# Ten weight subtractions move to GpSimd and the softmax's division to ScalarE, in a two-layer diffusion trunk

## The chip, the cores and the metric

One core of a Trainium2 chip runs the whole program. The metric is the time of one execution in device microseconds; the kernel before takes 1686.2 us as the median of three runs (1684.12 to 1688.48). Engines are named as in the profile: PE is TensorE (PEld its weight loads), DVE is VectorE, ACT is ScalarE, POOL is GpSimd, SP is SyncE, which here issues the DMAs.

## What is computed

Two layers work on 256 latent and 256 context tokens of width 1024. Each layer is a half-step SwiGLU feed-forward, a token mixer, and another half-step feed-forward, each behind an RMSNorm that is modulated by a conditioning vector. The change lies in the mixer:

```python
ux = modulate(rms_norm(h, norm_g[l, 1]), mx[:, 3], mx[:, 4])     # latent; uc: the same for context
px = ux @ w_in[l]                                                # one projection for all head groups
...
mix_x = concatenate([
    multiscale_pool(px[..., :HYENA_OFF], ...),                   # 256 wide: pooling
    hyena_mixer(px[..., HYENA_OFF:Q_OFF], ...),                  # 256 wide: long convolution
    blocked_attention(qx, k_all, v_all),                         # 8 heads of 64, 2 key/value heads
]) @ w_out[l]
...
def attend(q, k, v):
    s = einsum('bqkgd,bskd->bkgqs', q, k) * ATTN_SCALE
    p = softmax(s, axis=-1)
    o = einsum('bkgqs,bskd->bqkgd', p, v)
```

Latent queries attend to latent and context keys (512), context queries to context keys alone (256). In the last layer the context's own mixer output is not needed, so that only its keys and values are made.

## The kernel before

Products are made exact to about fp32 from three faster ones (`mm3`, lines 58 to 65): each operand is held as a high part and a low part (operand minus high part), and PE runs high x high, high x low and low x high into one PSUM bank. For weights, `Stream` does this on the way (lines 95 to 132). SP loads a unit of 128x1024 into one of three `raw` tiles (wr, line 107), ACT copies it rounded into one of four `whi` tiles (wh, line 117), DVE subtracts into one of three `wlo` tiles (wl, line 122), and then the load four units further on is issued. `ahead` and `take` say how far this runs ahead of the matmuls. There are 310 such units; those of the input projection follow `JOBS[l]`: three Hyena blocks whose projection is the `head` (line 418), and behind them q, k and v blocks ("qkv", two units each), the remaining Hyena blocks and the two pooling blocks (`bulk`, line 935).

In the head, the matmuls over the modulated activations run first over the first stream of tokens and then over the second. Their high parts yhb are made on ACT (line 341) and their low parts ylb on DVE (line 348). Where a mixer begins, POOL writes the tables of the rotary positions, tab0 and tab1 (line 707), each in three sets of four operations.

Behind the head run the Hyena convolutions (to_time with its copies u and x on ACT, line 776; U, Y, Ye, yo, lines 785 to 839), the norms and rotations of q and k (hsqq, hqq, hrq, lines 873 to 895, on DVE), the pooling sums on POOL (lines 739 to 757) and attention (line 1006). One item of attention is one head and 128 queries: PE makes the scores S (line 966), DVE the negated row maximum (mx, line 973), ACT the exponential with the row sums (e and sm, line 976), DVE the reciprocal and the division in place (lines 980 and 981), PE four or two transposes (St, line 986), ACT one half of the copy out of PSUM and DVE the other (pT, lines 991 and 993), PE the products with v (po, line 999), and ACT and DVE split them into high and low. An item's exponential, the division of the item before it and the transposes of the item four earlier stand together in the code.

Inside the mixers a scheduler sets the order of the instructions on each engine from its own estimates; head and tails are ordered by hand. Each engine works through its own instructions strictly in that order. Layer 0 has 32 items (16 with 512 keys, 16 with 256), layer 1 has 16 with 512.

Of the kernel before, what the change touches and what calls it, by code (L numbers as in the profile page):

```python
# [11 lines left out]
F32 = mybir.dt.float32  # L12
F32R = mybir.dt.float32r
I32 = mybir.dt.int32
AF = mybir.ActivationFunctionType
ALU = mybir.AluOpType
# [3 lines left out]
P = 128  # L20
# [13 lines left out]
def hymba(ctx: ExitStack, tc: tile.TileContext, io: dict, out: bass.AP):  # L34
    nc = tc.nc
# [59 lines left out]
    class Stream:  # L95


        def __init__(self, units):
            self.units = units
            self.raw, self.hi, self.lo = [], [], []  # L100
            self.taken = 0

# [7 lines left out]
        def ahead(self, n, more=0):  # L110

            end = min(self.taken + n + more, len(self.units))
            for i in range(len(self.hi), end):
                self.load(i + 1)
                m = self.units[i].shape[-1]
                hi = wp.tile([P, 1024], F32R, tag="whi", name=f"wh{i}", bufs=4)
                nc.scalar.activation(hi[:, :m], self.raw[i][:, :m], AF.Copy)  # L117
                self.hi.append(hi)
            for i in range(len(self.lo), min(self.taken + n, len(self.units))):
                m = self.units[i].shape[-1]  # L120
                lo = wp.tile([P, 1024], F32R, tag="wlo", name=f"wl{i}", bufs=3)
                self.last = nc.vector.tensor_tensor(lo[:, :m], self.raw[i][:, :m], self.hi[i][:, :m].bitcast(F32), ALU.subtract)  # L122
                self.lo.append(lo)
                self.load(i + 4)

# [522 lines left out]
    def mixers(l, nrm, fill):  # L648
# [329 lines left out]

        def normalise(e, sm, nk):
            nc.vector.reciprocal(sm, sm)  # L980
            nc.vector.tensor_scalar(e[:, :nk * P], e[:, :nk * P], sm, None, ALU.mult)

        def transposed(e, pT, nm, qb, nk):
            ps = bank(f"St{nm}")
# [21 lines left out]
        def attention(heads):  # L1006
# [10 lines left out]
            for i in range(len(items) + depth + 1):  # L1017
                if i < len(items):
                    yield from need("k", f"q{items[i][0]}")
                    if i % 2 == 0:  # L1020
                        j, s, a, qb, keys = items[i]
                        pss = scores(j, s, qb, keys)
                    es[i] = softmax(pss[i % 2], *items[i])
                if 0 < i <= len(items):
                    normalise(*es[i - 1], len(items[i - 1][4]))
                for d in due:
                    values(*d)
                due = []
                if 0 <= i - depth < len(items):
                    j, s, a, qb, keys = items[i - depth]  # L1030
                    nk = len(keys)
                    if (j, s) not in pTs:
                        pTs[j, s] = [[big(f"pT{l}{j}{s}{b}{n}") for n in range(nk // 2)] for b in range(2)]
                    transposed(es.pop(i - depth)[0], pTs[j, s][a], f"{l}{j}{s}{a}{qb}", qb, nk)
                    if a == 1 and qb == 1:
                        due.append((j, s, keys, pTs[j, s]))
                yield
# [25 lines left out]
    def mix_out(l, mix, S, nxt, fill):  # L1063
# [17 lines left out]
    JOBS = (  # L1081
        [("hy", 2), ("hy", 3), ("hy", 4), ("hy", 5), ("qkv", 1), ("qkv", 0), ("qkv", 2), ("hy", 6), ("hy", 7), ("pool", 0), ("pool", 1)],
        [("hy", 2), ("hy", 3), ("hy", 4), ("qkv", 0), ("hy", 5), ("qkv", 1), ("qkv", 2), ("hy", 6), ("hy", 7), ("pool", 1), ("pool", 0)],
    )
    NB0 = 6
    units = []
    for l in range(DEPTH):
        for s in range(2):
            units += [io["w_gu"][l, s, f, a] for f in range(NF) for a in range(2)][0 if l or s else NB0:]
            units += [io["w_down"][l, s, m, :, a * P:b * P] for m in range(KB) for a, b in ((0, 8), (8, 15), (15, NF))]  # L1090
            if s == 0:
                for kind, b in JOBS[l]:
                    units += [io["w_qkv"][l, b, i] for i in range(2)] if kind == "qkv" else [io["w_feat"][l, b]]
                units += [io["w_out"][l, m] for m in range(KB)]
    weights = Stream(units)

    def start():

# [336 lines left out]
```

## Time and profile before

| | |
|---|---|
| runs, median (lowest, highest) | 1686.2 us (1684.12, 1688.48) |
| the profiled execution, its time and its span | 1689.82 us, 1688.0 us |
| PE, DVE, ACT, POOL busy | 1640.8, 1168.9, 873.1, 91.9 us |
| mean granted clock of PE | 0.989 |

The chain of work that ended last gives PE 86% and DVE 10% of the span. In a timeline a row is a run of instructions of one kind: when it starts, how long it lasts, and in brackets how long its engine stood idle before it and which instruction let it go. In a window row each engine has its busy time in that stretch and its number of instructions; PEclk is the granted clock, 1.00 being full speed. The mixers of layer 0 lie between about 430 and 580 us, those of layer 1 between about 1355 and 1463.

### The profile page before, as it was taken

How to read it: one execution, taken by the hardware profiler on the slowest of the kernel's cores; microseconds unless marked ns; L12 is line 12 of the kernel's file. 1: busy time of each engine (PE TensorE's matmuls, PEld its weight loads, DVE VectorE, ACT ScalarE, POOL GpSimd, SP SyncE). 2: the span in 40 equal slices, each digit the busy share in tenths (PEclk: the TensorE clock that was granted, in tenths of full speed). 3: DMA queues.
4: the chain of work that ended last, by engine and by line, in shares of the span. 5: the costliest groups of instructions: out<-in, count | busy, mean ns of one | idle time of the engine just before them, and what ended most of it. 6: DMA issues, size and time to landing. Idle time of an engine off the chain costs nothing.

```text
span 1688.0 us, 24751 instructions
## 1 busy us (share of the span) xinstructions
PE 1640.8 (97%) x9162; PEld 1398.6 (83%) x9162; DVE 1168.9 (69%) x2107; ACT 873.1 (52%) x1881; POOL 91.9 (5%) x120
## 2 busy tenths in 40 slices
PE   7999999999999999999999999999999995999999
PEld 5687788888897698888888898888888895789999
DVE  5688778666789767767633368777765698776653
ACT  3576567655424635656522236666655543454442
POOL 0222200000102100000000000000000012000000
PEclk9999999999999999999999999999999998999999
DMA  9455455555421024545433325555555452345564
GB/s 337 129 186 185 135 189 188 172 171 168 142 75 40 24 76 139 173 153 169 158 89 101 95 73 188 176 185 187 174 164 155 133 184 82 125 150 180 184 185 139
DMA packets 80121, 251.50 MB, mean 149 GB/s; under 512 B 8641, under 2 KB 14145, under 8 KB 80001
## 3 DMA queue, kind: packets, MB, share of 16 engines
q1 hardware_dynamic: 80000, 249.93, 45.9%
q8 instruction: 72, 1.18, 0.3%
q14 instruction: 49, 0.39, 0.1%
HBM read 246.75 MB, written 3.15 MB: 148 GB/s over the span
## 4 chain that ended last, share of the span: by engine, by line
PE 86%; DVE 10%; ACT 1%; issue 1%; DMA 1%; POOL 1%; SPq 0%; ACTq 0%; DVEq 0%; POOLq 0%
PE fp L63 15%; PE fp L64 15%; PE fp L65 15%; PE fd L63 7%; PE fd L65 7%; PE fd L64 7%; PE fp L429 2%; DVE wl L122 1%; PE po L999 1%; PE op L63 1%; PE op L64 1%; PE op L65 1%; PE St L986 1%; PE ip L429 1%; PE qp L862 1%
## 5 line engine op out<-in xcount | busy, mean ns | idle before, releaser
L117 ACT ACTIVATE wh<-wr 128x1024 fp32r<-128x1024 f32 (+1 forms) x310 | 320.6, 1036 | 483.3 <-PE fp L64 171.9
L122 DVE TENSOR_TENSOR wl<-wr,wh 128x1024 fp32r<-128x1024 f32 (+1 forms) x310 | 371.4, 1199 | 215.4 <-PE fd L65 92.8
L63 PE MATMUL fp<-yha,wh 128*128 128x512 f32 x632 | 251.0, 397 | 0.0
L65 PE MATMUL fp<-yha,wl 128*128 128x512 f32 x632 | 247.0, 391 | 0.0
L64 PE MATMUL fp<-yla,wh 128*128 128x512 f32 x632 | 247.0, 391 | 0.0
L63 PE MATMUL fd<-gh,wh 128*128 128x512 f32 (+1 forms) x616 | 223.3, 362 | 0.0
L64 PE MATMUL fd<-gl,wh 128*128 128x512 f32 (+1 forms) x616 | 223.3, 362 | 0.0
L65 PE MATMUL fd<-gh,wl 128*128 128x512 f32 (+1 forms) x616 | 223.3, 362 | 0.0
L63 PE MATMUL fp<-yhc,wh 128*128 128x512 f32 (+1 forms) x656 | 220.5, 336 | 0.0
L64 PE MATMUL fp<-ylc,wh 128*128 128x512 f32 (+1 forms) x656 | 220.4, 336 | 0.0
L65 PE MATMUL fp<-yhc,wl 128*128 128x512 f32 (+1 forms) x656 | 220.4, 336 | 0.0
L202 ACT ACTIVATE mt<-mt 128x512 f32<-128x512 f32 x240 | 149.9, 626 | 127.1 <-DVE mt L201 124.8
L201 DVE TENSOR_TENSOR mr<-mr,cb 128x512 f32<-128x512 f32 x240 | 159.7, 706 | 0.0
L201 DVE TENSOR_TENSOR mt<-mr,cb 128x512 f32<-128x512 f32 x240 | 159.6, 702 | 0.0
L202 ACT ACTIVATE mr<-mr 128x512 f32<-128x512 f32 x240 | 147.7, 617 | 5.3 <-DVE mr L201 5.0
L63 PEld LDWEIGHTS fp<-yha,wh 128*128 128x128 f32 x632 | 119.3, 189 | 30.2 <-issue 2.0
L64 PEld LDWEIGHTS fp<-yla,wh 128*128 128x128 f32 x632 | 119.3, 189 | 26.4 <-issue 1.9
L65 PEld LDWEIGHTS fp<-yha,wl 128*128 128x128 f32 x632 | 119.2, 189 | 25.1
L65 PEld LDWEIGHTS fp<-yhc,wl 128*128 128x128 f32 x656 | 124.5, 190 | 12.9
L64 PEld LDWEIGHTS fp<-ylc,wh 128*128 128x128 f32 x656 | 124.5, 190 | 12.7
L63 PEld LDWEIGHTS fp<-yhc,wh 128*128 128x128 f32 x656 | 124.5, 190 | 12.6
L65 PEld LDWEIGHTS fd<-gh,wl 128*128 128x128 f32 x616 | 116.3, 189 | 18.1
(521 smaller groups left out, 2640.1 us busy)
## 6 DMA issues: line engine op xcount, KB each, us to landing
wr<-in_w_gu SPq DMA_DIRECT2D x170, 512.0 KB, 3.5
mr<-in_w_modT SPq DMA_DIRECT2D x120, 512.0 KB, 3.5
wr<-in_w_down SPq DMA_DIRECT2D x64, 448.0 KB, 3.4
wr<-in_w_down SPq DMA_DIRECT2D x32, 512.0 KB, 3.6
m0w<-in_w_mod SPq DMA_DIRECT2D x32, 256.0 KB, 5.6
wr<-in_w_feat SPq DMA_DIRECT2D x16, 512.0 KB, 3.7
wr<-in_w_out SPq DMA_DIRECT2D x16, 512.0 KB, 3.4
wr<-in_w_qkv SPq DMA_DIRECT2D x12, 512.0 KB, 3.7
```

The source lines that it names most:

```text
L63: nc.tensor.matmul(ps, w[0], x[0], start=start, stop=False)
L64: nc.tensor.matmul(ps, w[0], x[1], start=False, stop=False)
L65: nc.tensor.matmul(ps, w[1], x[0], start=False, stop=stop)
L117: nc.scalar.activation(hi[:, :m], self.raw[i][:, :m], AF.Copy)
L122: self.last = nc.vector.tensor_tensor(lo[:, :m], self.raw[i][:, :m], self.hi[i][:, :m].bitcast(F32), ALU.subtract)
L201: nc.vector.tensor_tensor(ta, ra, cb[:, c, a * 512:(a + 1) * 512], ALU.mult)
L202: nc.scalar.activation(ta, ta, AF.Copy, accum_out=acc[:, k, c, a:a + 1])
L429: nc.tensor.matmul(pss[b][:, cols(s)], w[:, k * P:(k + 1) * P], y[k][p[1]][:, cols(s)], start=(p == HH and k == 0), stop=(b in last and k ...
L862: nc.tensor.matmul(o_, x[0][:, ct], w[1][:, cw], start=False, stop=(k == KB - 1))
L986: nc.tensor.transpose(ps[:, i * P:(i + 1) * P], e[:, i * P:(i + 1) * P], ident)
L999: nc.tensor.matmul(po[a * HD:(a + 1) * HD, :SEQ], att["v"][:, kb, a * HD:(a + 1) * HD], pT[a][n // 2][:, cols(n % 2)], start=(n == 0), sto ...
```

## The change

Two things. `Stream` gets a set `beside` of unit numbers whose low part is subtracted on POOL in place of DVE. The set holds every second unit of the input projection behind the head, five a layer: qkv 1a, qkv 0a, qkv 2a, hy 6 and pool 0 in layer 0, qkv 0b, qkv 1a, qkv 2a, hy 6 and pool 1 in layer 1. And the division of the softmax (48 items) becomes a copy on ACT whose scale is the reciprocal column; the reciprocal stays on DVE.

```diff
--- before.py
+++ after.py
@@ -95,8 +95,10 @@
     class Stream:
 
 
-        def __init__(self, units):
+
+        def __init__(self, units, beside):
             self.units = units
+            self.beside = beside
             self.raw, self.hi, self.lo = [], [], []
             self.taken = 0
 
@@ -119,7 +121,10 @@
             for i in range(len(self.lo), min(self.taken + n, len(self.units))):
                 m = self.units[i].shape[-1]
                 lo = wp.tile([P, 1024], F32R, tag="wlo", name=f"wl{i}", bufs=3)
-                self.last = nc.vector.tensor_tensor(lo[:, :m], self.raw[i][:, :m], self.hi[i][:, :m].bitcast(F32), ALU.subtract)
+                if i in self.beside:
+                    nc.gpsimd.tensor_tensor(lo[:, :m], self.raw[i][:, :m], self.hi[i][:, :m].bitcast(F32), ALU.subtract)
+                else:
+                    self.last = nc.vector.tensor_tensor(lo[:, :m], self.raw[i][:, :m], self.hi[i][:, :m].bitcast(F32), ALU.subtract)
                 self.lo.append(lo)
                 self.load(i + 4)
 
@@ -978,7 +983,7 @@
 
         def normalise(e, sm, nk):
             nc.vector.reciprocal(sm, sm)
-            nc.vector.tensor_scalar(e[:, :nk * P], e[:, :nk * P], sm, None, ALU.mult)
+            nc.scalar.activation(e[:, :nk * P], e[:, :nk * P], AF.Copy, scale=sm)
 
         def transposed(e, pT, nm, qb, nk):
             ps = bank(f"St{nm}")
@@ -1084,15 +1089,18 @@
     )
     NB0 = 6
     units = []
+    beside = set()
     for l in range(DEPTH):
         for s in range(2):
             units += [io["w_gu"][l, s, f, a] for f in range(NF) for a in range(2)][0 if l or s else NB0:]
             units += [io["w_down"][l, s, m, :, a * P:b * P] for m in range(KB) for a, b in ((0, 8), (8, 15), (15, NF))]
             if s == 0:
+                n0 = len(units) + 3
+                beside.update(range(n0 + 1, n0 + sum(2 if kind == "qkv" else 1 for kind, _ in JOBS[l][3:]), 2))
                 for kind, b in JOBS[l]:
                     units += [io["w_qkv"][l, b, i] for i in range(2)] if kind == "qkv" else [io["w_feat"][l, b]]
                 units += [io["w_out"][l, m] for m in range(KB)]
-    weights = Stream(units)
+    weights = Stream(units, beside)
 
     def start():
```

The scheduler then sets a new order. On POOL at the start of layer 0's mixers (gs0q and gs0k are factors of the rope tables, tab0... the tables, pu a pooling buffer, wl a low part), before:

```order
47 L701 TENSOR_SCALAR gs0q<-mc_2_3813 128x128
48 L701 TENSOR_SCALAR gs0k<-mc_2_3813 128x128
49 L707 TENSOR_TENSOR tab0qcos<-mc_1_3812,gs0q 128x2x64 x4
50 L707 TENSOR_TENSOR tab0qsin<-mc_1_3812,gs0q 128x2x64 x4
51 L707 TENSOR_TENSOR tab0k<-mc_1_3812,gs0k 128x2x64 x4
52 L739 MEMSET pu_00_4890 128x8
53 L740 MEMSET pu_00_4890 128x8
```

and now:

```order
47 L706 TENSOR_SCALAR gs0q<-mc_2_3813 128x128
48 L706 TENSOR_SCALAR gs0k<-mc_2_3813 128x128
49 L125 TENSOR_TENSOR wl_4046<-wr_3834,wh_4040 128x1024
50 L712 TENSOR_TENSOR tab0qcos<-mc_1_3812,gs0q 128x2x64 x4
51 L712 TENSOR_TENSOR tab0qsin<-mc_1_3812,gs0q 128x2x64 x4
52 L712 TENSOR_TENSOR tab0k<-mc_1_3812,gs0k 128x2x64 x4
53 L125 TENSOR_TENSOR wl_4158<-wr_4044,wh_4095 128x1024
54 L125 TENSOR_TENSOR wl_4353<-wr_4099,wh_4291 128x1024
55 L125 TENSOR_TENSOR wl_4510<-wr_4240,wh_4461 128x1024
56 L125 TENSOR_TENSOR wl_4700<-wr_4410,wh_4633 128x1024
57 L744 MEMSET pu_00_4890 128x8
58 L745 MEMSET pu_00_4890 128x8
```

The subtraction wl_4046 stands ahead of the rope tables, four more behind them; in layer 1 wl_12177 stands in the same way ahead of tab1 and the four others behind.

On ACT in layer 1, where the Hyena convolution's input goes to the time layout (u and x are copies of the transposed tt1u and tt1x, wh the high copies of weights), before:

```order
1039 L117 ACTIVATE wh_12545<-wr_12440 128x1024
1040 L873 ACTIVATE hsqq_12500<-qp_1_0_12448 128x512
1041 L117 ACTIVATE wh_12600<-wr_12446 128x1024
1042 L117 ACTIVATE wh_12664<-wr_12543 128x1024
1043 L776 ACTIVATE u_0_12532<-tt1u_12527 128x512
1044 L776 ACTIVATE x_0_12539<-tt1x_0_12534 128x512
1045 L55 ACTIVATE tfk1h<-tfk_12602 128x512
1046 L787 ACTIVATE Uo1a_12617<-U1a_1_12611 128x512
```

and now:

```order
1070 L878 ACTIVATE hsqq_12500<-qp_1_0_12448 128x512
1071 L119 ACTIVATE wh_12600<-wr_12446 128x1024
1072 L781 ACTIVATE u_0_12532<-tt1u_12527 128x512
1073 L781 ACTIVATE x_0_12539<-tt1x_0_12534 128x512
1074 L119 ACTIVATE wh_12664<-wr_12543 128x1024
1075 L55 ACTIVATE tfk1h<-tfk_12602 128x512
1076 L792 ACTIVATE Uo1a_12617<-U1a_1_12611 128x512
```

The copies u and x now stand before wh_12664.

On ACT in layer 0's attention (e_5451 the exponentials of an item, pT transposed ones), before:

```order
459 L976 ACTIVATE e_5451,sm_5452<-S_5416,mx_5449 128x512
460 L991 ACTIVATE pT_5444<-St_5456 128x2x128
461 L991 ACTIVATE pT_5443<-St_5475 128x2x128
462 L991 ACTIVATE pT_5444<-St_5486 128x2x128
463 L976 ACTIVATE e_5470,sm_5471<-S_5460,mx_5468 128x512
```

and now:

```order
482 L981 ACTIVATE e_5451,sm_5452<-S_5416,mx_5449 128x512
483 L996 ACTIVATE pT_5444<-St_5456 128x2x128
484 L981 ACTIVATE e_5470,sm_5471<-S_5460,mx_5468 128x512
485 L986 ACTIVATE e_5451<-e_5451,sm_5452 128x512
486 L996 ACTIVATE pT_5443<-St_5475 128x2x128
487 L981 ACTIVATE e_5481,sm_5482<-S_5461,mx_5479 128x512
488 L986 ACTIVATE e_5470<-e_5470,sm_5471 128x512
489 L996 ACTIVATE pT_5444<-St_5486 128x2x128
```

Each division (an ACTIVATE that writes and reads the same e) stands behind its exponential with one or two other instructions between them.

## Rows read from the trace of the kernel before

**Rows 1.** The page: busy times, chain by engine, and the subtraction's group.

```profile
PE 1640.8 (97%) x9162; PEld 1398.6 (83%) x9162; DVE 1168.9 (69%) x2107; ACT 873.1 (52%) x1881; POOL 91.9 (5%) x120
...
PE 86%; DVE 10%; ACT 1%; issue 1%; DMA 1%; POOL 1%; SPq 0%; ACTq 0%; DVEq 0%; POOLq 0%
...
L122 DVE TENSOR_TENSOR wl<-wr,wh 128x1024 fp32r<-128x1024 f32 (+1 forms) x310 | 371.4, 1199 | 215.4 <-PE fd L65 92.8
```

**Rows 2.** PE's timeline, layer 0: start, length, work xcount [idle before <-releaser].

```profile
437.93 0.62 PE L429 MATMUL ip<-ylb,wh 128*128 128x256 f32 x3 [0.77 <-DVE ylb L348]
...
439.35 1.68 PE L429 MATMUL ip<-ylb,wh 128*128 128x256 f32 x9 [0.80 <-DVE ylb L348]
...
441.55 1.21 PE L429 MATMUL ip<-yhb,wl 128*128 128x256 f32 x8 [0.30 <-DVE wl L122]
...
547.70 0.39 PE L966 MATMUL S<-tfk0h,tfq011h 64*128 64x256 f32 x2 [1.02 <-DVE mx_4l L56]
...
578.32 1.35 PE L999 MATMUL po<-pT,vs 128*64 128x256 f32 x8 [0.77 <-ACT pT L991]
```

**Rows 3.** Windows of layer 0's mixers, all engines.

```profile
core 0: us, PE busy (x) PEld busy (x) DVE busy (x) ACT busy (x) POOL busy (x), PEclk, DMA share, GB/s
...
500.00:520.00 20.00, 20.00 (x102) 16.09 (x101) 19.40 (x45) 8.61 (x14) 0.15 (x2) 1.00 0.32 101
...
540.00:560.00 20.00, 16.81 (x112) 10.15 (x112) 19.82 (x54) 14.02 (x47) 13.48 (x21) 1.00 0.09 27
...
531.70:577.50 45.80, 41.37 (x305) 27.69 (x304) 44.10 (x128) 32.69 (x106) 19.40 (x30) 1.00 0.04 13
```

**Rows 4.** PE's timeline, layer 1, its five longest mixer waits in order.

```profile
1360.79 0.62 PE L429 MATMUL ip<-ylb,wh 128*128 128x256 f32 x3 [0.77 <-DVE ylb L348]
...
1362.21 1.05 PE L429 MATMUL ip<-ylb,wh 128*128 128x256 f32 x4 [0.81 <-DVE ylb L348]
...
1396.26 2.71 PE L785 MATMUL U1a<-u,dft 128*128 128x256 f32 x8 [2.19 <-ACT u L776]
...
1418.33 0.66 PE L904 MATMUL tfq<-ca,hqq 128*128 128x128 f32 x2 [7.00 <-DVE hqq L895]
...
1434.11 1.19 PE L839 MATMUL yo<-idft,Ye1b 128*128 128x128 f32 x4 [7.22 <-DVE Ye1b L800]
```

**Rows 5.** Windows of layer 1's mixers, columns as in rows 3.

```profile
1400.00:1420.00 20.00, 13.00 (x97) 12.61 (x96) 18.97 (x41) 6.57 (x10) 5.93 (x10) 0.84 0.32 107
...
1420.00:1440.00 20.00, 12.25 (x64) 9.34 (x62) 14.65 (x33) 5.25 (x15) 3.14 (x5) 0.80 0.00 0
...
1438.40:1460.00 21.60, 21.42 (x148) 13.35 (x145) 19.69 (x55) 14.77 (x44) 0.00 (x0) 1.00 0.52 171
```

**Rows 6.** POOL's groups by shape: xcount, busy us, mean ns, idle before.

```profile
L612 POOL TENSOR_TENSOR fab<-fab,fab 128x512 f32<-128x512 f32 x4 | 5.6, 1396 | 0.0
```

**Rows 7.** POOL's timeline in the filters of the start.

```profile
105.50 5.86 POOL L610 TENSOR_TENSOR fpq<-fd 128x256 f32<-128x256 f32 x1 [16.11 <-DVE fd L605]
```

**Rows 8.** Line 348: duration ns min/median/max, first and last start.

```profile
L348 DVE SCALAR_TENSOR_TENSOR ylb<-ntb,mod,yhb x32: 475/478/765, 432.4 to 1372.4; 128x256 fp32r<-128x256 f32 x32
```

**Rows 9.** ACT's timeline in the head and bulk of layer 1.

```profile
1369.02 2.49 ACT L341 ACTIVATE yhb<-ntb,mod 128x256 fp32r<-128x256 f32 x6
...
1394.66 1.06 ACT L117 ACTIVATE wh<-wr 128x1024 fp32r<-128x1024 f32 x1 [1.49 <-DMA wr<-in_w_feat]
```

**Rows 10.** Line 981, the division, as rows 8.

```profile
L981 DVE TENSOR_SCALAR e<-e,sm x48: 336/477/872, 514.0 to 1458.3; 128x512 f32<-128x512 f32 x32, 128x256 f32<-128x256 f32 x16
```

**Rows 11.** The page's groups: an activation in SBUF, 128x512.

```profile
L202 ACT ACTIVATE mr<-mr 128x512 f32<-128x512 f32 x240 | 147.7, 617 | 5.3 <-DVE mr L201 5.0
```

**Rows 12.** ACT's groups by shape from 531.7 to 577.5: the exps of layer 0.

```profile
L976 ACT ACTIVATE e<-S,mx 128x512 f32<-128x512 f32 x13 | 9.0, 705 | 4.1 <-DVE mx L973 2.2 <-DVE sm L980 1.9
...
L976 ACT ACTIVATE e<-S,mx 128x256 f32<-128x256 f32 x16 | 7.7, 480 | 3.3 <-DVE mx L973 2.7 <-DVE sm L980 0.5
```

**Rows 13.** The same from 1438.4 to 1460: the exps of layer 1.

```profile
L976 ACT ACTIVATE e<-S,mx 128x512 f32<-128x512 f32 x12 | 8.3, 690 | 4.3 <-DVE mx L973 2.7 <-DVE sm L980 1.6
```

## The prediction

> **What bounds the kernel now.** I read the page first, its chain of waits, then the table of windows through the two mixer stretches, and last PE's own timeline for its waits. Over the whole span PE is busy 97% and the chain is 86% PE and 10% DVE [rows 1]; so a lighter DVE is worth something only where PE stands still for it. Those places lie in the two mixers, some 260 of 1688 us. Layer 0: PE waits three times for the second stream's ylb and a wl, 1.87 us together, then nothing over 1.4 us until attention, where it waits about 1 us at a time for DVE (one of those waits is shown) [rows 2]. In attention DVE is the fullest engine: 19.82 of 20 us from 540 to 560 and 44.10 of 45.80 over the stretch from the first to the last of 29 exps, in which PE is busy 41.37 and ACT 32.69 [rows 3]. Layer 1: PE waits 0.77 and 0.81 for ylb, 2.19 for ACT's u, 7.00 for DVE's hqq and 7.22 for Ye1b [rows 4], and its granted clock is 0.84 and 0.80 in the two windows of the long waits; the attention after them keeps PE full, 21.42 of 21.60 [rows 5].
>
> **Part one, ten subtractions from DVE to POOL.** One costs DVE 1.20 us [rows 1]. POOL takes 1.40 us for a two-input operation on 128x512 [rows 6], so about 2.8 for one on 128x1024 by doubling (an estimate). The row on the bad side is a 128x256 operation that took 5.86 us while DVE was busy beside it [rows 7], over four times what the 128x512 one takes; so 2.8 to some 7. DVE pays as well: ylb takes 0.478 us as a rule and 0.765 at most [rows 8], the long ones while POOL writes the rope tables. At that ratio DVE work that runs beside a 2.8 us subtraction loses 2.8 x (1 - 0.478/0.765) = 1.05 us, nearly the 1.20 that it saves. So I take the moved subtractions at about nothing for DVE's load where DVE is full, and only their side effects in the order count:
> - The first moved subtraction stands ahead of the rope tables on POOL in both layers. The weights for it come only once the projection is under way, so the twelve operations that write the tables slide behind it and no longer run beside ylb of the second stream. ylb goes back to 0.478 and PE's waits for it go: -1.87 us in layer 0 and -1.58 in layer 1 [rows 2, 4]. I take them whole; the bounds are 0 (DVE, relieved, still late) and these sums. The tables themselves are wanted only by the rotary products, which come after the first q and k projections (hqq in layer 1 ends at 1418 [rows 4]), and that covers the delay.
> - In layer 1 the first moved low part is ready 1.6 us later than on DVE (2.8 for 1.2), or 5.8 at the other end, and PE comes to it soon after; I take +0.4, bounds 0 and +3. The other nine have several us of PE work ahead of them.
> - In layer 1 ACT now makes u and x before the high copy that waited 1.49 us for its DMA and took 1.06 [rows 9]; before, u stood behind it. PE's 2.19 us wait for u goes but for a remainder of 0.1: -2.1. The copy itself is not needed by PE for several us. Bounds -2.19 and 0.
> - The waits for hqq and Ye1b I leave: in the order the subtractions that remain on DVE, not the moved ones, stand between hqq's inputs and hqq. If the relief does reach them, they shrink by up to three subtractions, 3.6 us (a rival, below).
>
> The Trainium skill ("SBUF — State Buffer", "Who interferes with whom") says that a GpSimd operation that reads SBUF and a VectorE one with two SBUF inputs exclude each other for a whole instruction. The trace agrees in direction (0.765 for 0.478), though that is less than a full exclusion of the long operation. By that rule each moved subtraction would hold DVE for 2.8 us where it saves 1.2; it is the third rival.
>
> **Part two, 48 divisions from DVE to ACT.** DVE loses 0.477 us each (median) [rows 10], about 14 us of its 44.10 in layer 0's attention. It is then far from full and its waits there go. ACT gets them. No row shows a Copy with a per-partition scale: from below, a 128x512 activation in SBUF without such a column takes 0.617 us [rows 11] and from above the exp with its bias column 0.705 [rows 12]; for 128x256 six activations with a bias column took 2.49 us, 0.415 each [rows 9], and the exp takes 0.480 [rows 12]. In a full queue ACT's instructions overlap a little, so I take the lower rows: 0.61 and 0.41. In the stretch from 531.7 to 577.5 there are 13 exps of 512 and 16 of 256 [rows 12], and so 13 x 0.61 + 16 x 0.41 = 14.5 us more. ACT's 32.69 become 47.2 us of work in a stretch that lasted 45.80: ACT becomes the fullest engine, past PE's 41.37 [rows 3]. With the upper prices (0.705 and 0.48) it is 49.5, with overlap in the rest of the queue as well perhaps 46.
>
> How full can such an engine run? DVE as the bound got 44.10 / 45.80 = 96.3% in the same stretch [rows 3]. ACT's queue has a round trip in every item (exp, reciprocal on DVE, division), but the order puts another exp or copy between an exp and its division in nearly all items, and PE transposes an item only three items later. I take 96.3%: 47.2 / 0.963 = 49.0 us, +3.2 against 45.80. Layer 1's attention: 14.77 + 12 x 0.61 = 22.1 us of ACT in 21.60 [rows 5, 13]; at 96.3% 22.9, +1.3. DVE waits of PE that vanish inside these stretches are not counted again: they are part of the 45.80 that ACT's time replaces. The last steps (copy, po, split) stay as they are: ACT's pT already released the last of them [rows 2].
>
> **Sum.** Layer 0: -1.87 + 3.2 = +1.3. Layer 1: -1.58 + 0.4 - 2.1 + 1.3 = -2.0. Together -0.7 us on the profiled execution's 1689.82 (span 1688.0 and 1.8 outside), 1689.1. That execution is 3.6 us above the median of the runs, 1686.2, so I forecast 1685.5.
>
> **Rivals.**
> - *ACT's queue stalls (slower).* Place: attention, above all layer 0. Every division waits for a reciprocal and holds up the exps and copies behind it, on which PE depends. For it: ACT would be at its limit without any stall; ACT's idle time in attention now is largely spent waiting for DVE's max and reciprocal (4.1 us before the 13 exps) [rows 12]. Against: DVE has 14 us less to do there. At 85% full: 47.2 / 0.85 = 55.5, +9.7; layer 1 26.0, +4.4; with the gains of the heads and u, -1.87 - 1.58 + 0.4 - 2.1 = -5.15, it is +9 us, 1695. It comes out slower than can be told from no change when ACT runs below some 89% (53.0 and 24.8, +10.4 - 5.15).
> - *Relief goes further (faster).* ACT runs without gaps (47.2 and 22.1: +1.4 and +0.5) and the three subtractions taken off DVE ahead of hqq shorten its wait by 3.6: 1.9 - 5.15 - 3.6 = -6.9, 1679.3. For it: DVE is 18.97 of 20 us busy from 1400 to 1420, and the low granted clock there would rise with fewer gaps [rows 5]. Against: the order ahead of hqq.
> - *POOL and DVE block each other.* Each of the three subtractions of layer 0 that fall after 480 costs DVE 2.8 - 1.2 = 1.6 net, 4.8 us, just where it begins to be late; PE would wait that much longer for the first items; layer 1 loses another 3 on late low parts. -0.7 + 4.8 + 3 = +7, 1693. For it: the 5.86 [rows 7]. Against: PE is busy all of 500 to 520 [rows 3], so the lateness falls in a stretch where nobody waits, and DVE has the room of the divisions to catch up. Half of that cost, +3.2, is as likely as the whole. In the skill's words ("Perfetto Trace Analysis", "Optimizing Scalar/DVE Operations") moving work between these two engines "might not help".
>
> **How the numbers follow.** Forecast 0.56; ACT stalls 0.18; further relief 0.16; mutual blocking 0.10. The forecast's own range: ACT full to between 100% and 90% (layer 0 +1.4 to +6.6, layer 1 +0.5 to +3.0) less 5.15 gives -3.3 to +4.5 on the median, 1683 to 1691. What a measurement of this kernel can tell from no change is about 0.3%, 5 us: 1681.1 to 1691.3. Faster: the second rival and a little of the forecast, 0.18. Slower: the first rival and half of the third, 0.23. No change 0.59. The 8-in-10 range reaches to the second rival and to the first, 1678.5 to 1695.
>
> **What would show it.** Right: no PE wait for ylb of the second stream and none over 0.5 for u; ACT above 44 us busy over attention of layer 0, DVE near 32, PE's waits there put down to ACT; that stretch 47 to 51 us long. Wrong: divisions on ACT well over 0.61 or under 0.5; ACT idle more than 10% there with PE waiting; POOL subtractions over 4 us, or PE waiting for a wl made on POOL; hqq's wait clearly under 6 us; the first ylb waits still there because the first moved subtraction came too early or too late.

## The result: 0.9% slower, and the profile after

The changed kernel takes 1702.2 us as the median of four runs (1699.05 to 1704.03), the one before 1687.3 beside it: a ratio of 1.0087, with a 95% interval of 1.0063 to 1.0111. The forecast was 1685.5 us with a range up to 1695.

The page of the kernel after, its busy times and its chain by engine, against [rows 1]:

```profile
PE 1638.8 (97%) x9162; PEld 1396.4 (82%) x9162; DVE 1151.8 (68%) x2049; ACT 898.0 (53%) x1929; POOL 113.8 (7%) x130
...
PE 86%; DVE 7%; ACT 3%; issue 2%; DMA 1%; POOL 1%; SPq 0%; POOLq 0%; DVEq 0%; ACTq 0%
```

DVE has 17 us less work, ACT 25 and POOL 22 more; 3% of the chain is now ACT. PE's timeline in layer 0 (columns as in [rows 2], which it answers):

```profile
433.21 0.61 PE L434 MATMUL ip<-yhb,wh 128*128 128x256 f32 x3 [0.17 <-ACT yhb L346]
...
483.34 0.48 PE L867 MATMUL qp<-wl,yhb 128*128 128x256 f32 x1 [4.03 <-DVE wl L127]
...
538.32 0.79 PE L971 MATMUL S<-tfk0h,tfq011h 64*128 64x512 f32 x1 [1.66 <-DVE pT L998]
...
548.15 0.65 PE L1004 MATMUL po<-pT,vs 128*64 128x256 f32 x2 [1.33 <-ACT pT L996]
...
573.31 0.65 PE L1004 MATMUL po<-pT,vs 128*64 128x256 f32 x2 [1.79 <-ACT pT L996]
...
583.77 1.35 PE L1004 MATMUL po<-pT,vs 128*64 128x256 f32 x8 [0.93 <-ACT pT L996]
```

The waits for ylb are gone, as forecast. In their place stands a wait of 4.03 us for a low part that DVE still makes, and in attention four of over 0.9 us (three are shown) in which ACT's copy pT comes late. PE's products po over attention of layer 0, before and after, with the idle time before them:

```profile
L999 PE MATMUL po<-pT,vs 128*64 128x256 f32 x96 | 14.2, 391 | 2.7 <-DVE pT L993 1.9 <-ACT pT L991 0.8
```

```profile
L1004 PE MATMUL po<-pT,vs 128*64 128x256 f32 x96 | 16.7, 432 | 5.9 <-ACT pT L996 5.9
```

PE waits 5.9 us for ACT's pT there, where it waited 0.8.

In layer 1, against [rows 4]:

```profile
1370.35 0.39 PE L867 MATMUL qp<-wl,yhb 128*128 128x256 f32 x1 [0.56 <-POOL wl L125]
...
1393.18 0.60 PE L778 MATMUL tt1x<-ca,zc 128*128 128x128 f32 x3 [3.49 <-DVE zc L731]
...
1423.46 0.66 PE L909 MATMUL tfq<-ca,hqq 128*128 128x128 f32 x2 [10.18 <-DVE hqq L900]
...
1440.34 1.20 PE L844 MATMUL yo<-idft,Ye1b 128*128 128x128 f32 x4 [7.49 <-DVE Ye1b L805]
```

ylb's and u's waits are gone here too; zc's 3.49 us are new, and PE waits 10.18 us for hqq where it waited 7.00 (subs_only, below, has 7.38). Behind the longer wait stands an earlier hqq, an instruction of 0.68 us as a rule, which began beside POOL's last subtraction; from it to the hqq that PE waits for DVE has no gap over 0.15 us:

```profile
1400.56 2.88 DVE L900 TENSOR_TENSOR hqq<-hqq,hrq 128x512 f32<-128x512 f32 x1
...
1399.66 3.22 POOL L125 TENSOR_TENSOR wl<-wr,wh 128x1024 fp32r<-128x1024 f32 x1 [8.03 <-PE qp L867]
```

Windows over attention of layer 0, from its second group of transposes to the output projection, columns as in [rows 3]: the whole piece before, then the whole after and fifths of it.

```profile
535.60:579.60 44.00, 39.59 (x286) 25.74 (x286) 40.59 (x119) 30.25 (x100) 17.65 (x26) 1.00 0.04 13
```

```profile
530.90:585.10 54.20, 45.30 (x287) 27.68 (x287) 30.95 (x91) 44.61 (x132) 16.61 (x29) 0.94 0.03 10
...
530.90:541.70 10.80, 8.36 (x50) 5.81 (x52) 9.41 (x25) 7.80 (x24) 7.50 (x14) 0.83 0.12 44
...
541.70:552.60 10.90, 9.57 (x58) 5.57 (x54) 3.81 (x12) 8.07 (x23) 8.02 (x15) 0.85 0.00 1
...
552.60:563.40 10.80, 9.69 (x65) 5.68 (x65) 6.83 (x21) 10.65 (x31) 1.10 (x2) 1.00 0.01 2
...
563.40:574.30 10.90, 8.91 (x66) 5.56 (x62) 7.43 (x23) 10.59 (x33) 0.00 (x0) 1.00 0.00 1
...
574.30:585.10 10.80, 8.76 (x60) 5.06 (x58) 3.46 (x12) 7.50 (x25) 0.00 (x0) 1.00 0.01 2
```

ACT has 44.61 us of work in 54.20: full in the middle (10.65 of 10.80, 10.59 of 10.90), 69 to 74% busy at both ends. PE's granted clock is 0.94 over the piece (0.83 and 0.85 in its first two fifths) for 1.00 before. Of the 10.2 us that the piece grew by, PE is idle for 4.5 and busy for 5.7. What the clock alone costs is not separated; it can't be the main cause, since in the whole attention of layer 0 subs_only lost nothing at 0.96 and div_only lost 8.2 us at 0.97.

The two profiled executions don't start alike: in the one before, the clock granted in the first 200 us was 0.97 and 0.95, and it reached the mixers 6.7 us later than the one after (1.00). So spans are not compared below. Instead the mixers are cut into six pieces by the first instructions of their kind on PE: head (first ip, the input projection, to first tt0u or tt1u), bulk (from there to attention's first St in layer 0, first S in layer 1) and attention (from there to the first op, the output projection); 0 and 1 are the layers. Their lengths before are 26.8, 75.7, 47.2, 33.8, 36.3 and 38.4 us. What each kernel adds, worked out from its start times, with its median over that of the kernel before run beside it:

```
us more than before  head0 bulk0 att0  head1 bulk1 att1   sum   median, and of before
the change            -2.5  +5.0  +9.6  -3.2  +3.6  +3.3  +16.0  1702.2  1687.3
subs_only             -2.5  +5.9   0.0  -3.1  +2.2   0.0   +2.4  1689.6  1688.1
div_only               0.0  -0.1  +8.2  -1.0  +2.4  +3.0  +12.5  1699.5  1688.1
first_only            -2.5  -0.5   0.0  -3.1  +1.4  +0.3   -4.5  1683.5  1688.1
half_div              +0.1  -0.1  +2.6  -1.0  +2.4  +0.1   +4.1  1691.1  1688.1
subs_memset           -2.5  -0.4   0.0  -3.4  -3.0  +0.4   -9.0  1676.9  1688.1
subs_twice            -2.5  +9.7  +0.3  +2.4  +9.1  +0.2  +19.2  1703.6  1688.1
tables_late           -2.4  -0.1   0.0  -3.4  +1.2  +0.2   -4.4  1681.2  1688.1
div_depth5            +0.9  +1.9 +13.4  -0.2  +1.9  +2.5  +20.5  1704.5  1688.1
dummy_act              0.0  -0.1 +11.4  -1.0  +1.3  +1.8  +13.4  1703.7  1688.9
div_pt_dve            +1.2  -0.1  +6.8  -1.0  +1.2  +4.7  +12.8  1701.7  1688.9
tl_div_early          -2.4  -0.1  +2.1  -3.4  -1.2   0.0   -5.0  1683.9  1688.9
tl_pool_late          -2.4  -0.1   0.0  -3.3  -2.6  +0.1   -8.2  1679.5  1687.6
```

The sums follow the medians within some 4 us. Of one run's bulk1 some 2 us are not the kernel's: it holds the stretch of low granted clock [rows 5], and in runs that keep all low parts on DVE it lies anywhere from -1.2 (tl_div_early) to +2.4 (div_only, half_div) of the kernel before, -1.2 and +1.2 in tl_div_early and tables_late, whose second layers are the same. A head can differ by 1 us for the same reason: head1 of the kernel before ran at a granted clock of 0.95, that of div_only, which leaves the tables alone, at 1.00 and 1.0 us shorter; head0 of div_pt_dve ran at 0.94. In div_depth5 16 matmuls moved from att0 into bulk0.

### The profile page after: what moved, and what is told of

It reads as the page before. It is cut to its first block, busy times and chain, and to the rows that moved or that the text cites. A ratio compares the mean times of both kernels' runs of the same rounds, so it can differ in the third digit from the quotient of the medians.

```text
span 1697.3 us, 24748 instructions
## 1 busy us (share of the span) xinstructions
PE 1638.8 (97%) x9162; PEld 1396.4 (82%) x9162; DVE 1151.8 (68%) x2049; ACT 898.0 (53%) x1929; POOL 113.8 (7%) x130
## 4 chain that ended last, share of the span: by engine, by line
PE 86%; DVE 7%; ACT 3%; issue 2%; DMA 1%; POOL 1%; SPq 0%; POOLq 0%; DVEq 0%; ACTq 0%
PE fp L63 15%; PE fp L64 15%; PE fp L65 15%; PE fd L63 7%; PE fd L64 7%; PE fd L65 7%; PE fp L434 2%; PE po L1004 1%; DVE wl L127 1%; PE ip L434 1%; ACT e L981 1%; PE op L63 1%; PE op L64 1%; PE op L65 1%; PE qp L867 1%
## 5 line engine op out<-in xcount | busy, mean ns | idle before, releaser
L127 DVE TENSOR_TENSOR wl<-wr,wh 128x1024 fp32r<-128x1024 f32 (+1 forms) x300 | 360.6, 1202 | 210.4 <-PE fd L65 94.3
L65 PEld LDWEIGHTS fp<-yhc,wl 128*128 128x128 f32 x656 | 124.5, 190 | 12.9
```

The source lines that it names most:

```text
L65: nc.tensor.matmul(ps, w[1], x[0], start=False, stop=stop)
```

## The experiments

**subs_only** and **div_only** split the change.

```diff
 subs_only:
-            nc.scalar.activation(e[:, :nk * P], e[:, :nk * P], AF.Copy, scale=sm)
+            nc.vector.tensor_scalar(e[:, :nk * P], e[:, :nk * P], sm, None, ALU.mult)
 div_only:
-                beside.update(range(n0 + 1, ...))
+                pass
```

> The ten subtractions on POOL, the division back on DVE. Theory A (a DVE instruction that reads SBUF and begins beside a POOL subtraction stands until that is done, and in attention ACT has too much work): the heads still gain some 3 us a layer, the stalls of 2 us each on DVE make PE wait about 4 us for a low part (qp, layer 0) and 3.5 us for zc in layer 1, attention goes back to its old length: about 1687 to 1692. Theory B (the whole loss is ACT's, the subtractions pay): both waits are gone or under 1 us and the time is 1679 to 1683.

> All low parts on DVE as before, the division on ACT. Theory A (ACT's added work itself): attention of layer 0 is 8 to 10 us longer, that of layer 1 about 3, no wait for low parts: 1698 to 1702. Theory B (attention is long because DVE comes late to it after the POOL subtractions, and PE's clock falls): attention grows by under 4 us together: 1687 to 1692.

Measured: 1689.6 us, ratio 1.0012 (1.0000 to 1.0024), and 1699.5, ratio 1.0068 (1.0052 to 1.0084). Together +12.8 us of the +14.9: the parts add up to within some 2 us. Both theories A hold. With the subtractions alone both waits are there (4.04 and 3.49 us) and both attentions have their old length. With the division alone neither wait is there and attention grows by 8.2 and 3.0 us, so the length of attention does not come from what the subtractions do ahead of it.

**first_only** leaves one subtraction a layer on POOL.

```diff
-                beside.update(range(n0 + 1, n0 + sum(...), 2))
+                beside.add(n0 + 1)
```

> Only the first of the five subtractions a layer on POOL, ahead of the rope tables; the division on DVE. Theory A (the heads' gain comes from the tables that no longer run beside ylb, and the loss from the other four): 1680 to 1684, PE's waits for ylb in the heads gone, no wait of 2 us or more for a low part. Theory B (the gain in the heads is used up later, where DVE's chain sets the end): 1686 to 1689.

Measured: 1683.5 us, ratio 0.9977 (0.9964 to 0.9991), theory A. The heads gain all that they gain in the change (-2.5 and -3.1), the wait of 4 us is gone. So the other eight subtractions cost some 7 us in bulk0 and bulk1 (subs_only against this run: 6.4 and 0.8, the latter within what bulk1 varies by; 6.1 in the medians).

**subs_memset** and **subs_twice** change only what POOL does in those ten places.

```diff
 subs_memset:
-                    nc.gpsimd.tensor_tensor(lo[:, :m], self.raw[i][:, :m], self.hi[i][:, :m].bitcast(F32), ALU.subtract)
+                    nc.gpsimd.memset(lo[:, :m].bitcast(F32), 0.0)
 subs_twice:
+                    nc.gpsimd.tensor_tensor(lo[:, :m], self.raw[i][:, :m], self.hi[i][:, :m].bitcast(F32), ALU.subtract)
```

> As the run with the ten subtractions alone, but POOL fills those ten low parts with zeros in place of subtracting (their share of the products is left out); DVE and PE have the same instructions in the same order. Theory A (DVE stands because POOL's subtraction reads SBUF): the DVE instructions of 2.4 to 2.9 us are 0.7 or less, PE's waits of 4.04 and 3.49 us go under 1 us, 1681 to 1684. Theory B (the order of DVE's instructions makes its low part late): the waits and the time stay, 1688 to 1691.

> As the run with the ten subtractions alone, but POOL does each of them twice; DVE, PE and ACT have the same instructions in the same order. Theory A (DVE stands for as long as POOL's subtraction lasts): the four or five long DVE instructions may come twice, each 2 us more; PE's wait for the low part in layer 0 grows from 4.0 to 6 to 9 us, layer 1 by 2 to 5: 1694 to 1700. Theory B: only the low parts made on POOL are 2.4 us later, which PE notices once: 1690 to 1693.

Measured: 1676.9 us (0.9933, 0.9919 to 0.9946), 1689.6 and 1703.6 (1.0091, 1.0075 to 1.0106) for none, one and two readings by POOL, with one order on DVE and PE: 13 and 14 us for each step, so theory A, and both ends lie even beyond what it expected. DVE's timeline shows how. Two instructions on the path to the low part that PE waits for, in the runs with the filling, with one and with two subtractions (start, length):

```profile
467.64 0.69 DVE L805 TENSOR_TENSOR Ye0a<-Y0a,Y0a 128x512 f32<-128x512 f32 x1
...
478.61 0.68 DVE L800 TENSOR_TENSOR U0a<-U0a,kf 128x512 f32<-128x512 f32 x1
```

```profile
467.76 2.76 DVE L805 TENSOR_TENSOR Ye0a<-Y0a,Y0a 128x512 f32<-128x512 f32 x1
...
480.81 2.58 DVE L800 TENSOR_TENSOR U0a<-U0a,kf 128x512 f32<-128x512 f32 x1
...
485.19 1.21 DVE L127 TENSOR_TENSOR wl<-wr,wh 128x1024 fp32r<-128x1024 f32 x1
...
467.21 2.77 POOL L125 TENSOR_TENSOR wl<-wr,wh 128x1024 fp32r<-128x1024 f32 x1 [9.76 <-PE qp L867]
...
480.45 2.40 POOL L125 TENSOR_TENSOR wl<-wr,wh 128x1024 fp32r<-128x1024 f32 x1 [10.47 <-PE qp L867]
...
486.46 0.58 PE L867 MATMUL qp<-wl,yhb 128*128 128x256 f32 x1 [4.04 <-DVE wl L127]
```

```profile
466.21 2.76 DVE L806 TENSOR_TENSOR Ye0a<-Y0a,Y0a 128x512 f32<-128x512 f32 x1
...
480.12 2.17 DVE L800 TENSOR_TENSOR Y0a<-U0a,kf 128x512 f32<-128x512 f32 x1
...
482.81 2.23 DVE L801 TENSOR_TENSOR U0a<-U0a,kf 128x512 f32<-128x512 f32 x1
...
488.10 0.58 PE L868 MATMUL qp<-wl,yhb 128*128 128x256 f32 x1 [6.51 <-DVE wl L128]
```

An instruction of 0.69 us that begins beside POOL's subtraction comes to its end only about half a microsecond after that one's: Ye0a from 467.76 to 470.5, where POOL's runs from 467.21 to 470.0. The two stalls are 2.07 and 1.90 us long, 3.97 together, and PE waits 4.04 us for the wl of 485.19, which had no time to spare before. While POOL only writes (0.95 us each), no DVE instruction is stretched; that is not for the filling's being short, since an U0a of the usual 0.69 us begins and ends inside one:

```profile
480.48 0.69 DVE L800 TENSOR_TENSOR U0a<-U0a,kf 128x512 f32<-128x512 f32 x1
...
480.25 0.97 POOL L125 MEMSET wl<- 128x1024 f32 x1 [12.29 <-PE qp L867]
```

**tables_late** leaves all subtractions on DVE and moves only the rope tables.

```diff
                 gs = sp.tile([P, 2, HD], F32, tag="gs" + nm, name=f"gs{l}{nm}", bufs=2)
+                nc.gpsimd.tensor_copy(gs[:, 0, 0:1], nrm.y[KB - 1][1][:, 0:1].bitcast(F32))
```

> No subtraction on POOL, division on DVE, but the rope tables wait for the last ylb of the second stream's predecessor (a one-column copy on POOL reads it first). Theory A (the gain in the heads is that the tables no longer run beside ylb): as with the first subtraction alone or slightly better, 1681 to 1684, PE's waits for ylb in both heads gone. Theory B (it is the subtraction less on DVE ahead of the low parts that counts): 1686 to 1688.

Measured: 1681.2 us, ratio 0.9958 (0.9946 to 0.9971), theory A. The heads' gain, -2.4 and -3.4, is that of the tables' place; what POOL does instead has no part in it.

**tl_pool_late** uses the same rule in a place of which the change says nothing.

```diff
+                if l == 1 and s == 0:
+                    while ("hq", 2) not in att:
+                        yield
+                    nc.gpsimd.tensor_copy(uv[:, 0:1], att["hq", 2][0][:, 0, 0, 0:1])
                 nc.gpsimd.memset(uv[:, 0:8], 0.0)
```

> The rope tables late, and in layer 1 POOL's pooling sums wait for the last q rotation (hqq) by a one-column copy, so that they no longer run beside hrq and hqq, for which PE waits 7.1 us; DVE, PE and ACT have the same instructions in the same order. Theory A (DVE instructions with two SBUF inputs stand for POOL's): hrq goes from 2.2 us for four back to 0.9, hqq to 0.7, PE's wait to 5.5: 1 to 2 us less than the tables late alone, 1679 to 1681. Theory B (that chain's end is set elsewhere, or Ye1b comes as late as before): within 0.5 us of it.

PE's and DVE's timelines of it, where tables_late has a wait of 7.12, hrq 2.20 and hqq 0.89:

```profile
1406.68 0.66 PE L914 MATMUL tfq<-ca,hqq 128*128 128x128 f32 x2 [5.62 <-DVE hqq L905]
...
1404.65 0.89 DVE L904 TENSOR_TENSOR hrq<-hsqq,tab1qsin 128x128 f32<-128x128 f32 x4
...
1405.85 0.68 DVE L905 TENSOR_TENSOR hqq<-hqq,hrq 128x512 f32<-128x512 f32 x1
```

The waits move as theory A says, by 1.50 us, and bulk1 is 3.8 us shorter than with the tables late alone, of which the wait explains 1.5; the rest is no more than this piece varies by. In the ratios the two kernels don't part: 1679.5 us, ratio 0.9958 (0.9944 to 0.9973). Both beat the kernel before and the change.

**half_div** has every second division on ACT.

```diff
+            if act:
+                nc.scalar.activation(e[:, :nk * P], e[:, :nk * P], AF.Copy, scale=sm)
+            else:
+                nc.vector.tensor_scalar(e[:, :nk * P], e[:, :nk * P], sm, None, ALU.mult)
...
+                    normalise(*es[i - 1], len(items[i - 1][4]), i % 2 == 0)
```

> All low parts on DVE, every second division on ACT, the other on DVE. Theory A (ACT's added work is what counts, in proportion beyond its room): ACT has some 39 us of work in a layer-0 attention of 46, DVE 37: attention is as long as before or up to 3 us shorter, 1683 to 1688. Theory B (a division in ACT's queue blocks what stands behind it, each costs alike): half of the division's loss, 1693 to 1696.

Measured: 1691.1 us, ratio 1.0027 (1.0016 to 1.0039), between the two. In layer 1 eight divisions cost 0.1 us and sixteen 3.0; in layer 0 sixteen cost 2.6 and 32 cost 8.2. The price is not in proportion: the second half costs twice the first or more, as for an engine that runs out of room, but in layer 0 it begins well before ACT is full (37.58 of 46.20 us busy in the piece shown above).

**dummy_act** keeps the division on DVE and gives ACT as much useless work.

```diff
             nc.vector.tensor_scalar(e[:, :nk * P], e[:, :nk * P], sm, None, ALU.mult)
+            nc.scalar.activation(scrap, e[:, 0:256], AF.Copy, scale=ones[:, 0:1])
+            if nk == 4:
+                nc.scalar.activation(scrap[:, 0:16], e[:, 256:272], AF.Copy, scale=ones[:, 0:1])
```

> The kernel before (low parts and division on DVE) with one more copy per item on ACT, of the length of a division (128x256, and 128x16 on top for 512 keys), of the divided exponentials into a scrap tile that nobody reads. Theory A (the time of the divisions in ACT's queue is what attention grows by): attention of layer 0 is 6 to 10 us longer and the time 1696 to 1702, about as with the division. Theory B (what costs is that the item itself waits for a division on ACT: exponential, reciprocal, division, transposes in a ring): the copies fill ACT's gaps, 1688 to 1692.

Measured: 1703.7 us, ratio 1.0085 (1.0068 to 1.0101), theory A by the number, and more: attention of layer 0 grows by 11.4 us with as much work on ACT there as in div_only (46.7 us in both). But the copies are not free of a ring, as theory A has it: each reads exponentials that DVE has divided, and ACT's queue stands for them (from 528.8 to 587.5 us; last column idle time before the group, and its releasers):

```profile
L989 ACT ACTIVATE scrap<-e,ones 128x256 bf16<-128x256 f32 x29 | 15.0, 518 | 4.7 <-DVE e L988 4.3 <-DVE sm L987 0.4
```

So this run does not tell ACT's added work from waiting for DVE, and the 3 us by which it is slower than div_only can be those 4.7 us or the 14 us of work that DVE keeps. The change itself does tell them apart; its groups on ACT by shape from 525 to 586 us:

```profile
L986 ACT ACTIVATE e<-e,sm 128x512 f32<-128x512 f32 x13 | 9.9, 759 | 0.0
...
L981 ACT ACTIVATE e<-S,mx 128x512 f32<-128x512 f32 x13 | 9.3, 715 | 0.6 <-DVE mx L978 0.6
...
L986 ACT ACTIVATE e<-e,sm 128x256 f32<-128x256 f32 x16 | 8.3, 519 | 0.3 <-DVE sm L985 0.3
...
L981 ACT ACTIVATE e<-S,mx 128x256 f32<-128x256 f32 x16 | 7.9, 492 | 3.3 <-DVE mx L978 3.2
```

ACT waits 0.3 us in all for a reciprocal before a division. (The means of 759 and 519 ns contain overlap; the divisions at 554.24 and 547.11 start 0.40 and 0.62 us ahead of what follows them.)

**div_pt_dve** relieves ACT of its copies.

```diff
-                if i == 0:
+                if False:
                     nc.scalar.activation(dst, src, AF.Copy)
```

> Division on ACT alone, and the half of the pT copies that ACT made on DVE as well, so that ACT has some 36 us of work in layer 0's attention and DVE 42. Theory A (ACT's work fills attention): attention goes back to 44 to 47 us, 1686 to 1690. Theory B (the ring through ACT): some 3 us less than with the division alone, 1694 to 1698, PE still waiting for e.

Measured: 1701.7 us, ratio 1.0070 (1.0050 to 1.0091). Both theories miss. ACT is no longer full (39.1 us of 54.1), attention of layer 0 comes back by 1.4 us only and that of layer 1 gets longer by 1.7. Three of PE's waits, in the order of the timeline:

```profile
539.72 1.08 PE L1004 MATMUL po<-pT,vs 128*64 128x256 f32 x2 [1.22 <-DVE pT L998]
...
1463.85 0.65 PE L1004 MATMUL po<-pT,vs 128*64 128x256 f32 x2 [1.58 <-DVE pT L998]
...
1469.97 0.65 PE L1004 MATMUL po<-pT,vs 128*64 128x256 f32 x2 [1.57 <-DVE pT L998]
```

They are now waits for pT on DVE, where the copies stand behind maxima, splits and reciprocals.

**div_depth5** puts one more item between scores and transposes.

```diff
-            depth = 4
+            depth = 5
```

> The division on ACT alone, with one more item between an item's scores and its transposes (depth 5 for 4). Theory A (ACT's work fills attention): nothing to gain, 1697 to 1701. Theory B (copies that PE waits for stand in ACT's queue behind exponentials and divisions, and more distance hides that): PE's waits for pT shrink, 1690 to 1696.

Measured: 1704.5 us, ratio 1.0098 (1.0081 to 1.0115): slower than the division alone. Theory B falls; that it got worse is not explained by theory A either. PE waits 1.65, 1.90 and 1.30 us for pT and its granted clock over this attention is 0.89.

**tl_div_early** divides on ACT for eight items at the start of layer 0's attention, where ACT has room.

```diff
+                    normalise(*es[i - 1], len(items[i - 1][4]), l == 0 and i <= 8)
```

> The rope tables late, and the division on ACT for the first 8 items of layer 0 alone, where ACT has room (4.3 us busy of 8.8 at attention's start) and DVE is full. Theory A (it depends on whether ACT has room at that place): no loss or a gain up to 2 us against the tables late alone, 1679 to 1682. Theory B (each division on ACT costs its share of the division's loss, 0.25 us): 1683 to 1685.

Measured: 1683.9 us, ratio 0.9973 (0.9960 to 0.9985), which is 2.7 us behind tables_late in the medians and 1.9 when each is taken against the kernel before beside it: theory B by the number, though the two intervals overlap. Its trace points to another reason than ACT's queue, on DVE (below) and on PE behind it:

```profile
531.84 1.54 DVE L56 TENSOR_TENSOR mx_2l<-zc,mx_2h 128x256 fp32r<-128x256 f32 x2
...
533.30 1.82 DVE L56 TENSOR_TENSOR mx_3l<-zc,mx_3h 128x256 fp32r<-128x256 f32 x2
...
535.38 0.41 DVE L1002 COPY pT<-St 128x256 f32<-128x256 f32 x1
...
535.84 0.79 PE L972 MATMUL S<-tfk0h,tfq011h 64*128 64x512 f32 x1 [1.64 <-DVE pT L1002]
```

With the divisions gone from DVE, the scheduler put four splits of the Hyena output in a row ahead of a maximum and of the pT that PE's next scores wait for. Beside POOL's pooling sums they take 3.4 us; in tables_late, divided by other work, the four take 0.81, 0.41, 0.55 and 0.96. PE's granted clock over this attention is 0.93 (0.96 in tables_late); how much of the 2.1 us the wait makes and how much the clock is not separated.

## Why the prediction was wrong

- **The heads: right, and larger.** PE's waits for ylb went in both layers as forecast (-1.87 and -1.58); the pieces shrank by 2.5 and 3.2 us, of which 1.0 in head1 is the clock of the kernel before. tables_late shows that it is the tables. The prediction had the stream wrong: in the order of `head` these are the low parts of the first stream. Those of the second still run beside tab1 in the change, seven of them at 0.68 us, and PE does not wait for them.
- **u in layer 1: right, and filled up again.** The wait of 2.19 us is gone, and zc's of 3.49 stands in its place, since DVE comes to zc after two of the stalls. In the change these read (start, length; hssk is 128x8 and takes 0.16 in layer 0, at 486.59):

```profile
1383.49 2.41 DVE L276 TENSOR_SCALAR hssk<-hssk 128x8 f32<-128x8 f32 x1
...
1389.35 2.57 DVE L900 TENSOR_TENSOR hqk<-hqk,hrk 128x256 f32<-128x256 f32 x1
...
1392.55 0.48 DVE L731 SCALAR_TENSOR_TENSOR zc<-ip,ca,zc 128x255 f32<-128x255 f32 x1
...
1383.46 2.41 POOL L125 TENSOR_TENSOR wl<-wr,wh 128x1024 fp32r<-128x1024 f32 x1 [1.91 <-DVE rs_r L273]
...
1389.22 2.41 POOL L125 TENSOR_TENSOR wl<-wr,wh 128x1024 fp32r<-128x1024 f32 x1 [3.35 <-PE qp L867]
```

- **The moved subtractions at about nothing for DVE: the first step that failed.** It took the slowing of ylb beside the tables, 0.478 to 0.765, as a ratio and put it on a long subtraction. But a table operation lasts half a microsecond, and 0.29 us is what one added to a ylb; the subtraction lasts 2.4 and adds up to 2.25. In sum the ratio was not far off: six stretched DVE instructions lose some 11 us, where ten subtractions saved 12. What it hid is where they fall. The savings were spread over a DVE that PE hardly waited for there (without the stalls, in subs_memset, the ten bring 4.3 us against tables_late, about 2.5 of them u's wait); each stall falls whole on one instruction, and those of 2.09 and 1.91 us in layer 0 lay on the way to a low part that had no slack. "PE is busy all of 500 to 520, so the lateness falls in a stretch where nobody waits" missed 483. This is the third rival in its mechanism, to which 0.10 was given. That its price for layer 0 fits (bulk0 +5.0 for 4.8) is luck: it counted three stalls of 1.6 behind 480 that delay attention's first items; there were two of about 2, at 464 and 477, and the subtraction behind 480 (497.22) stretched nothing. In layer 1 its 3 us with u's -2.1 and the +0.4 make +1.3 for a measured +3.6, in a piece that varies from -1.2 to +2.4 in runs that leave the low parts alone. The +0.4 itself, for a low part made on POOL, was met: 0.56. The Trainium skill's sentence ("SBUF — State Buffer", "Who interferes with whom"), that whoever starts second stands until the first has finished, was weighed against rows that could not tell the two apart; these traces agree with it (2.76 against 0.69 us), and also with its remark that an operation that only writes does not do this (subs_memset).
- **"I take 96.3%": the second step that failed, and the larger.** ACT's added work was sized well: 14.5 us forecast, 14.36 measured (44.61 after, 30.25 before, on pieces of equal content), and the two prices of a division, 0.61 and 0.41, met to 0.01. But DVE's 96.3% was taken for what any engine reaches in this stretch. ACT's work comes in heaps: it is full for the middle two fifths and idle for a quarter and more at both ends, where it waits for DVE's maxima at first and for po at last, and it ran at 82%. Attention grew by 9.6 and 3.3 us for 3.2 and 1.3, and div_only, with the division alone, shows 8.2 and 3.0 of it. What holds PE up is ACT's half of the copies pT: po waits for it 0.8 us in layer 0 before, 3.5 with half the divisions on ACT, 5.9 in div_only and the change. The first rival named the place and nearly the price (85% full, +9.7 and +4.4); its reason, that a division waits for its reciprocal, is not what the change shows: 0.3 us in all.
- **The chances.** The rivals were treated as alternatives, one at a time. They were two independent costs on different engines in different pieces, and both came: -5.7 in the heads, +8.6 in the bulk, +12.9 in attention. Adding the first rival's +14.1 and the third's +7.8 to the forecast's -5.15 gives some 1703 on its 1686.2.

Open: what bounds attention with the division on ACT, at its ends and once ACT is no longer full. div_pt_dve and div_depth5 took away ACT's excess or the nearness of the items, and neither brought the time back. That the scheduler's order on DVE changes with the divisions is shown for one place (tl_div_early); whether it explains the rest was not tried.

## What to carry to other kernels

Before work is moved to an engine, cut the stretch into pieces and add the work to each piece: ACT, at 69% on the mean of layer 0's attention before, had no room for the added work where its queue is dense, and stood idle at both ends all the same. A subtraction moved from DVE to POOL does not go away for DVE if both read SBUF: count a stall of up to nearly the whole POOL instruction for each (five of the ten cost DVE 1.9 to 2.25 us, a sixth 0.8), and look for the chain that it may fall on. The other way round, the cheapest gain here (0.4%) was to keep short POOL work away from a stretch in which PE waits for DVE.

## What was not expected of the hardware

A DVE instruction on 128x8 elements, a multiplication by a constant with one input, took 2.41 us in place of 0.16 when it began 0.03 us after a POOL subtraction (1383.49 and 1383.46, above): neither its small size nor its single SBUF input kept it from the stall. Not every instruction with one SBUF input stands, though. A sum over elements (TENSOR_REDUCE) took its usual 0.67 us beside another subtraction:

```profile
499.23 0.67 DVE L879 TENSOR_REDUCE hssq<-hsqq 128x8 f32<-128x512 f32 x1
...
497.22 2.37 POOL L125 TENSOR_TENSOR wl<-wr,wh 128x1024 fp32r<-128x1024 f32 x1 [17.49 <-PE qp L867]
```

An instruction that reads PSUM (zc at 1379.24) took its usual 0.47 us although it began 0.10 us after POOL's subtraction of 1379.14 to 1381.55. POOL's 128x1024 subtraction takes 2.40 us where no DVE instruction holds it up, less than the 2.8 by doubling the 128x512 row; behind a DVE subtraction that had begun first (1399.43 to 1400.65) it took 3.22.
